# Opening of a two-layer diffusion-transformer kernel: key and value weights by feature quarter, modulation columns tile by tile, squares in two chains, decay table later

## The chip, the cores and the metric

The kernel runs on one core of a Trainium2 chip. A core has a matrix engine (TensorE, PE in the profile; PEld are its weight loads), three engines for elementwise work (VectorE is DVE, ScalarE is ACT, GpSimd is POOL), a queue engine that issues transfers (SyncE, SP) and 16 DMA engines. The metric is the device time of one launch in microseconds (us). Lower is better.

## The reference

Two layers over 512 latent tokens (x) with a prefix of 256 context tokens (ctx), model width 1024. Layer 0 mixes tokens with windowed grouped-query attention, layer 1 with a bidirectional retention; each is followed by a gated feed-forward stage. The part that this case is about is the head of layer 0: modulation from a condition vector, the modulated norm, and the projection to keys and values.

```python
def rms_norm(x, g):
    xf = x.astype(jnp.float32)
    y = xf * lax.rsqrt(jnp.mean(xf * xf, axis=-1, keepdims=True) + EPS)
    return (y * g.astype(jnp.float32)).astype(x.dtype)

def modulate(h, shift, scale):
    return h * (1 + scale) + shift

# windowed_gqa_sink
    q_x, k_x, v_x = jnp.split(h_x @ w_qkv, [qd, qd + kvd], axis=-1)
...
    k_c, v_c = jnp.split(h_c @ w_qkv[:, qd:], 2, axis=-1)
...
# bidir_retention
    log_g = jax.nn.log_sigmoid(decay_logit.astype(f32))
...
# reference
    c_act = jax.nn.silu(c)[:, None, :]
    cc_act = jax.nn.silu(c_ctx)[None, None, :]
    y_ctx = ctx
    for i in range(DEPTH):
        mx = jnp.split(c_act @ ada_w[i] + ada_b[i], 6, axis=-1)
        mc = jnp.split(cc_act @ ada_w[i] + ada_b[i], 6, axis=-1)
        h_x = modulate(rms_norm(x, norm1_g[i]), mx[0], mx[1])
        h_c = modulate(rms_norm(y_ctx, norm1_g[i]), mc[0], mc[1])
...
```

## The kernel before

Features lie on the 128 partitions, tokens on the free axis; the model width is eight feature tiles k = 0..7, and a *feature quarter* q is the pair 2q, 2q+1. Stream s = 0 is latent (512 columns), s = 1 context (256). Every float32 product is made of three matmuls, from a high part (a cast, on ScalarE) and a low part (the difference, on VectorE) of both operands: high by high, low weight by high, high weight by low.

The opening computes keys and values of all tokens, one feature quarter after the other, as their modulation comes. Its loads stand in SP's program order from line 334 on: four tiles of modulation weights for a quarter (`ada_quarter_load`), weight chunks for keys and values (`load_w`), the context stream, rope table, masks, the first query chunk, and the tiles of four later modulation units (`unit_load`, `UNITS` = 4, 5, 8, 6 at line 28; the first of them has buffers of its own). All modulation tiles and two of the weight chunks share eight buffers ("adan"), so a load waits until an earlier tile has been read. SP issues in program order; a load that waits holds what is behind it. Of the four chunks of 512 KB, chunk 0 and 1 hold the key weights of head pair 0 and 1 for all features, chunk 2 and 3 the value weights of the first and the last two feature quarters.

For TensorE, VectorE and ScalarE the order is written out by hand between line 469 and 517: within this block each of them runs its instructions in program order. Outside it a planner orders them, by priority.

- `stats0` (line 423, with `add_square` and `rms`): squares of the eight latent tiles on ScalarE, summed by seven additions on VectorE into one tile, then a matmul with ones, and from it the factor (`neg_half_rstd`, line 194: three ScalarE steps, two on VectorE at lines 199 and 200). Filler matmuls (`busy`, line 415) run meanwhile.
- `ada_quarter` (line 337): 64 matmul passes (line 345) give the modulation rows of a quarter in one PSUM bank; ScalarE copies them (348), `fill` runs, TensorE transposes twice (352), VectorE adds the bias and folds the gain (`columns`, 358, 359 and 114) for stream 0; the function it returns does stream 1.
- `hidden0` (line 429): scales two tiles (VectorE, 438), adds the shift into the high part (ScalarE, 439), then the low part (VectorE, 443). `between` runs ahead of the low parts.
- `split_w` (line 380) and `split_low` (384): high and low parts of a whole weight chunk.
- `keys` (line 445) and `values` (line 455): the matmuls of one quarter. For a quarter and a head pair, the latent keys are six passes of 512 columns, and there are two head pairs. A value tile is 128 tokens.
- `ada_unit` (line 311): as a quarter, for one later unit; passes at line 315.

The decay table of layer 1 (lines 787 to 809) is 21 small VectorE operations on 8 columns. It stands outside the hand-written block, behind two ScalarE steps. Layer 1 reads it. The first feed-forward stage (22 tiles f, in groups; `seven` computes one tile f from the third on) comes after layer 0's attention.

Of the kernel before, what the change touches and what calls it, by code (L numbers as in the profile page):

```python
# [9 lines left out]
F32R = mybir.dt.float32r  # L10
BF16 = mybir.dt.bfloat16
AF = mybir.ActivationFunctionType
ALU = mybir.AluOpType
# [36 lines left out]
def dit_kernel(ctx, tc, xT, cT, crow, small, consts, masks, tabs0, tabs1, jtab, adaQ, adaN, adaT, wst, out):  # L50
# [165 lines left out]
    def rms(s, c=slice(None), bank=pj, behind=()):  # L216
        y = ssq[s][:, c]
        n = y.shape[1]
        tot = bank()[:, :n]
        after(nc.tensor.matmul(tot, ones, y, start=True, stop=True), behind)  # L220
        return neg_half_rstd(y, t_sq(n), tot, D)
# [142 lines left out]


# [14 lines left out]
    def split_w(pool):  # L380
        wkv.append((T(pool, 1024, "whi", 2, F32R), T(pool, 1024, "wlo", 2, F32R)))
        nc.scalar.copy(wkv[-1][0], raw[len(wkv) - 1])

    def split_low():
        i = lows.pop(0)
        nc.vector.tensor_tensor(wkv[i][1], raw[i], wkv[i][0], op=sub)

    lows = [0, 1, 2, 3]
# [3 lines left out]
    load_w(rp, "wraw", 2)  # L392
    load_w(rp, "wraw", 2)
    load_w(st_p, "adan", 8)
    wq.append(ada_quarter_load(1))
    res0[1] = load_stream(1)
    load_w(st_p, "adan", 8)
    wq += [ada_quarter_load(2), ada_quarter_load(3)]
# [20 lines left out]
    def squares0(s):  # L419
        for k in range(KT):  # L420
            add_square(s, k, res0[s][k], tmp=(lambda n: T(st_p, 512, "hs", 3)[:, :n], lambda n: T(st_p, SC, "sc", 2)[:, :n])[s])

    def stats0(s):
        squares0(s)
        cond_silu(ccol)
        ln_exp_turn()
        rms(s, bank=pT)

    def hidden0(s, *ks, between=()):
        y, ts = ssq[s], []  # L430
        for k in ks:
# [13 lines left out]
    def keys(s, q):  # L445
        for j in range(2):
            o = kvx[j] if s == 0 else kvc[:, j * SC:(j + 1) * SC]
            for i, (a, b) in enumerate(((0, 0), (1, 0), (0, 1))):
                for k in (2 * q, 2 * q + 1):
                    last = nc.tensor.matmul(o, wkv[j][a][:, k * P:(k + 1) * P], h[s][k][b],  # L450
                                            start=k + i == 0 and (s == 0 or j == 0),
                                            stop=k == KT - 1 and i == 2, skip_group_check=s == 1)
        return last

    def values(s, q, tiles=None):
        first = None
        for t in tiles or ((0, 1, 2, 3), (4, 5))[s]:
            tok = slice((t - 4 * s) * P, (t - 4 * s) * P + P)
            o = kvv[t // 2][:, t % 2 * 256:t % 2 * 256 + 256]
            for k in (2 * q, 2 * q + 1):  # L460
                cs = slice((k % 4) * 256, (k % 4) * 256 + 256)
                (whi, wlo), (hi, lo) = wkv[2 + q // 2], h[s][k]
# [6 lines left out]
    with tc.manual_schedule(engines={mybir.EngineType.PE, mybir.EngineType.DVE, mybir.EngineType.Activation}):  # L469
        for n in (SX, SX, SX, SX, 256):  # L470
            busy(n)
        stats0(0)
        c1 = ada_quarter(0, wq[0], lambda: busy(256))
        split_w(st_p)
        busy(SX)
        hidden0(0, 0, 1, between=(split_low,))
        c1()
        split_w(st_p)
        split_low()
        keys(0, 0)  # L480
# [24 lines left out]
        c1()  # L505
# [288 lines left out]
    nc.vector.tensor_scalar(t2, t1, 2.0, None, op0=add)  # L794
    nc.vector.reciprocal(t2, t2)
    nc.vector.tensor_tensor(t1, t1, t2, op=mult)
    nc.vector.tensor_tensor(t2, t1, t1, op=mult)
    NTERM = 10
    nc.vector.tensor_scalar(t3, t2, 1.0 / (2 * NTERM + 1), None, op0=mult)
    for k in range(NTERM - 1, 0, -1):  # L800
# [1118 lines left out]
```

## Time and profile before

| | us |
|---|---|
| median of 3 runs | 1747.07 |
| lowest, highest run | 1746.09, 1747.19 |
| the profiled execution | 1746.2 |
| its span in the trace | 1744.4 |
| TensorE busy in it | 1712.7 (98%) |
| VectorE busy | 1350.5 (77%) |
| ScalarE busy | 846.3 (49%) |
| transfers | 203.54 MB, mean 117 GB/s |

A row of a timeline gives the start in us from the span's start, the length, the engine, the line of the kernel, the operation, the tile written and those read, the shape, a count where several instructions of a kind stand in a row, and in brackets the idle time before it with what ended it. A row of a table by stretches gives the stretch, then for each engine its busy time and number of instructions, then the TensorE clock that was granted (1.00 is full), the share of the DMA engines and GB/s. A row on waits gives engine and line, what it waited for, the total, the count and the longest. The chain of waits follows the work that ended last back through what released it. Matmuls overlap, so rows of TensorE are compared by their starts.

### The profile page before, as it was taken

How to read it: one execution, taken by the hardware profiler on the slowest of the kernel's cores; microseconds unless marked ns; L12 is line 12 of the kernel's file. 1: busy time of each engine (PE TensorE's matmuls, PEld its weight loads, DVE VectorE, ACT ScalarE, POOL GpSimd, SP SyncE). 2: the span in 40 equal slices, each digit the busy share in tenths (PEclk: the TensorE clock that was granted, in tenths of full speed). 3: DMA queues.
4: the chain of work that ended last, by engine and by line, in shares of the span. 5: the costliest groups of instructions: out<-in, count | busy, mean ns of one | idle time of the engine just before them, and what ended most of it. 6: DMA issues, size and time to landing. Idle time of an engine off the chain costs nothing.

```text
span 1744.4 us, 27605 instructions
## 1 busy us (share of the span) xinstructions
PE 1712.7 (98%) x10876; PEld 1527.8 (88%) x10876; DVE 1350.5 (77%) x2368; ACT 846.3 (49%) x1492; POOL 131.0 (8%) x270
## 2 busy tenths in 40 slices
PE   7999999999999999999999999999999999999999
PEld 5777777899999999999988888898898899999997
DVE  6697778788778788787889858758768798777774
ACT  5576667465433334342456534525525565445442
POOL 0035435000000000000000000000000000000000
PEclk9999999999999999999999999999999999999999
DMA  9501012533243534343423524423423224233322
GB/s 353 230 13 38 13 43 68 204 122 135 71 147 121 158 109 145 123 153 101 156 99 86 182 84 130 162 86 121 157 85 118 76 84 132 77 117 101 104 79 85
DMA packets 59602, 203.54 MB, mean 117 GB/s; under 512 B 6608, under 2 KB 6992, under 8 KB 59216
## 3 DMA queue, kind: packets, MB, share of 16 engines
q1 hardware_dynamic: 51984, 175.03, 30.9%
q0 software_dynamic: 7200, 26.22, 5.2%
q8 instruction: 85, 1.39, 0.3%
q10 hardware_dynamic: 288, 0.52, 0.1%
q14 instruction: 45, 0.37, 0.1%
HBM read 199.65 MB, written 2.10 MB: 116 GB/s over the span
## 4 chain that ended last, share of the span: by engine, by line
PE 80%; DVE 8%; DMA 5%; ACT 3%; issue 2%; POOL 1%; SPq 0%; ACTq 0%; POOLq 0%; DVEq 0%
PE Y L886 15%; PE Z L886 7%; PE pj L147 6%; PE pj L148 6%; PE pj L149 6%; PE Z L1268 6%; PE X L886 4%; PE Y L1257 3%; PE pj L1268 2%; PE pT L726 2%; PE X L1257 2%; DMA wraw<-in_wst_dram 2%; PE pO L740 2%; PE S L703 2%; DMA adan<-in_adaQ_dram 1%
## 5 line engine op out<-in xcount | busy, mean ns | idle before, releaser
L164 ACT CAST whi<-wraw 128x1024 fp32r<-128x1024 f32 x258 | 270.2, 1051 | 370.7 <-PE Z L149 88.5
L165 DVE TENSOR_TENSOR wlo<-wraw,whi 128x1024 fp32r<-128x1024 f32 x258 | 315.0, 1223 | 60.9 <-ACT whi L164 59.7
L886 PE MATMUL Y<-aq,whi 128*128 128x384 f32 x640 | 173.7, 335 | 0.5 <-ACT sq L1044 0.5
L256 DVE SCALAR_TENSOR_TENSOR res<-pj,mod,res 128x512 f32<-128x512 f32 (+1 forms) x112 | 81.5, 729 | 65.6 <-PE pj L149 65.0
L886 PEld LDWEIGHTS Y<-aq,whi 128*128 128x128 f32 x640 | 116.6, 188 | 1.7 <-ACT sq L1044 0.9
L273 DVE CUSTOM_DVE_ANT_0 y<-adaw,crow,small_sb 128x1024 bf16<-128x1024 f32 x64 | 81.9, 1280 | 36.0 <-DMA adaw<-in_adaT_dram 35.7
L886 PE MATMUL Y<-aq,wlo 128*128 128x384 f32 x320 | 107.0, 334 | 0.0
L101 ACT ACTIVATE pr<-pr,stat,qs 128x513 f32<-128x513 f32 (+2 forms) x96 | 74.4, 777 | 23.5 <-DVE stat L710 22.9
L1268 PE MATMUL Z<-whi,sA 128*128 128x512 f32 x256 | 81.0, 391 | 1.2 <-ACT gate L1454 1.2
L717 POOL TENSOR_SCALAR pr<-pr,stat 128x512 f32<-128x512 f32 (+2 forms) x96 | 70.2, 744 | 79.5 <-DVE stat L714 54.8
L147 PE MATMUL pj<-ax,whi 128*128 128x512 f32 x176 | 68.8, 391 | 0.1
L149 PE MATMUL pj<-ax,whi 128*128 128x512 f32 x176 | 68.7, 390 | 0.0
L148 PE MATMUL pj<-ax,wlo 128*128 128x512 f32 x176 | 68.5, 389 | 0.0
L147 PE MATMUL pj<-act,whi 128*128 128x512 f32 x168 | 66.0, 393 | 0.0
L148 PE MATMUL pj<-act,wlo 128*128 128x512 f32 x168 | 65.9, 392 | 0.0
L149 PE MATMUL pj<-act,whi 128*128 128x512 f32 x168 | 65.5, 390 | 0.0
L270 POOL DMA_DIRECT2D adaw<-in_adaT_dram x48 | 25.6, 533 | 514.9 <-DVE mod L273 413.6
L726 PE MATMUL pT<-const_sb,pr 128*128 128x128 f32 x352 | 57.4, 285 | 6.1 <-POOL pr L717 3.6
L886 PE MATMUL Y<-sA,whi 128*128 128x256 f32 x304 | 60.6, 282 | 0.2 <-ACT res L1721 0.2
L886 PEld LDWEIGHTS Y<-aq,wlo 128*128 128x128 f32 x320 | 60.1, 188 | 0.0
L726 PEld LDWEIGHTS pT<-const_sb,pr 128*128 128x128 f32 x352 | 39.1, 142 | 23.0 <-POOL pr L717 12.4
L1268 PEld LDWEIGHTS Z<-whi,sA 128*128 128x128 f32 x256 | 48.0, 188 | 11.7 <-ACT gate L1454 1.9
(576 smaller groups left out, 5150.3 us busy)
## 6 DMA issues: line engine op xcount, KB each, us to landing
wraw<-in_wst_dram SPq DMA_DIRECT2D x224, 512.0 KB, 3.7
adaw<-in_adaT_dram POOLq DMA_DIRECT2D x48, 512.0 KB, 3.9
wx<-in_wst_dram SPq DMA_DIRECT2D x30, 512.0 KB, 4.3
adan<-in_adaQ_dram SPq DMA_DIRECT2D x16, 512.0 KB, 8.5
adan<-in_adaN_dram SPq DMA_DIRECT2D x12, 512.0 KB, 7.8
adaw<-in_adaT_dram SPq DMA_DIRECT2D x8, 512.0 KB, 3.9
res<-in_xT_dram SPq DMA_DIRECT2D x14, 256.0 KB, 3.8
aq<-in_adaN_dram SPq DMA_DIRECT2D x12, 256.0 KB, 5.8
```

The source lines that it names most:

```text
L101: ins = nc.scalar.activation(*args, **kw)
L147: nc.tensor.matmul(o, whi, xhi, start=first, stop=False)
L148: nc.tensor.matmul(o, wlo, xhi, start=False, stop=False)
L149: return nc.tensor.matmul(o, whi, xlo, start=False, stop=last)
L164: after(nc.scalar.copy(hi, t), behind)
L165: return nc.vector.tensor_tensor(lo, t, hi, op=sub)
L256: return nc.vector.scalar_tensor_tensor(res[d], o, mods[l, s][:, part, d:d + 1], res[d], mult, add)
L273: res.append(nc.vector.tensor_tensor_reduce(junk, w, cr[:, s * 1024:(s + 1) * 1024], 1.0, sm_t[:, C_ADAB + l * 48 + j:C_ADAB + l * 48 + j ...
L726: nc.tensor.transpose(tp[:, a * P:(a + 1) * P], self.pr[(0, 2, 1, 3)[a]][:, ki * P:(ki + 1) * P], ident)
L886: nc.tensor.matmul(o, p, r, start=first and k + i == 0, stop=k == 3 and i == 2, skip_group_check=not first)
L1257: ins = nc.tensor.matmul(o[:, e * SC:(e + 1) * SC], p[:, ws], r, start=first and k + e + i == 0, stop=k == 3 and i == 2, skip_group_check= ...
L1268: ins = nc.tensor.matmul(os[t], p, r, start=first and k + i == 0, stop=k == 3 and i == 2, skip_group_check=by_k or not first)
```

## The change

1. `rms` can sum several tiles by ones (`rest`). `stats0` keeps two running sums, for even and odd tiles: six additions in place of seven, and two matmuls with ones. One short filler matmul is left out.
2. The key and value weights are stored by feature quarter: chunk q holds, for tiles 2q and 2q+1, the key weights of both head pairs (columns 0 to 511) and the value weights (512 to 1023). `split_high` and `split_low` take a column range; quarters 0 and 1 are split in halves (keys, values), quarters 2 and 3 whole.
3. The order of loads: quarter 0's modulation tiles, chunk 0, quarter 1's tiles, chunk 1, the context stream, quarter 2's tiles, chunk 2, quarter 3's tiles, chunk 3. Chunks 0 and 1 have buffers of their own, as the first two had; chunks 2 and 3 take one of the eight.
4. `ada_tiles` takes the place of `ada_quarter` for quarters 0 and 1: the quarter's two tiles one after the other, each with its 32 passes, its copy, a `fill` and its transpose, both transposes into one bank. The weights of these two quarters are stored to suit. Columns are added tile by tile, each ahead of its tile's scaling (`ahead` of `hidden0`).
5. `keys` can run part by part (`by_part`): all high passes, then all low-weight passes, then all low-hidden passes.
6. The hand-written order follows: the context squares stand behind the second quarter's low parts, the context factor in the fill of the third modulation quarter, two value tiles of quarter 1 ahead of it. `split_low(2)` stands where the last `split_low()` stood; `split_high(3)` behind the last latent `hidden0`, `split_low(3)` behind the last context one.
7. The VectorE part of the decay table becomes `decay`, called in the first feed-forward stage behind tile f = 12.

```diff
-    def rms(s, c=slice(None), bank=pj, behind=()):
+    def rms(s, c=slice(None), bank=pj, behind=(), rest=()):
...
-        after(nc.tensor.matmul(tot, ones, y, start=True, stop=True), behind)
+        for i, t in enumerate((y, *rest)):
+            after(nc.tensor.matmul(tot, ones, t, start=i == 0, stop=i == len(rest)), behind)
...
+    def ada_tiles(q, w, fill):
+        t = None
+        for d in range(2):
+            o = pT()[:, 0:P]
+            for k2 in range(4):
+                for j in range(4):
+                    k = 2 * k2 + j % 2
+                    nc.tensor.matmul(o[32 * j:32 * j + 32, :], ccol[:, k, :], w[2 * d + j // 2][:, k * P:(k + 1) * P],
+                                     start=k2 == 0, stop=k2 == 3)
+            rows = t_sq(P)
+            nc.scalar.copy(rows, o)
+            fill[d]()
+            if t is None:
+                t = pT()[:, 0:256]
+            nc.tensor.transpose(t[:, d * P:(d + 1) * P], rows, ident)
...
+        def columns(s, d0, d1):
+            col = mods[0, s][:, 0:2, 2 * q + d0:2 * q + d1]
+            nc.vector.tensor_tensor(col, tv[:, s, 0, :, d0:d1], bias[:, :, d0:d1], op=add)
+            nc.vector.tensor_tensor(col, tv[:, s, 1, :, d0:d1], col, op=add)
+            fold_gain(0, s, 0, 2 * q + d0, 2 * q + d1)
+
+        return columns
...
+    def split_high(q, c=slice(0, 1024)):
+        if q == len(wkv):
+            pool = (st_p, rp)[q // 2]
+            wkv.append((T(pool, 1024, "whi", 2, F32R), T(pool, 1024, "wlo", 2, F32R)))
+        nc.scalar.copy(wkv[q][0][:, c], raw[q][:, c])
+
+    def split_low(q, c=slice(0, 1024)):
+        nc.vector.tensor_tensor(wkv[q][1][:, c], raw[q][:, c], wkv[q][0][:, c], op=sub)
...
     load_w(rp, "wraw", 2)
+    wq.append(ada_quarter_load(1))
     load_w(rp, "wraw", 2)
-    load_w(st_p, "adan", 8)
-    wq.append(ada_quarter_load(1))
     res0[1] = load_stream(1)
-    load_w(st_p, "adan", 8)
-    wq += [ada_quarter_load(2), ada_quarter_load(3)]
+    for q in (2, 3):
+        wq.append(ada_quarter_load(q))
+        load_w(st_p, "adan", 8)
...
+    def stats0():
+        ssq[0] = t_y(0)
+        sums = ssq[0], t_sq(SX)
+        for k in range(KT):
+            sq = sums[k] if k < 2 else T(st_p, 512, "hs", 3)
+            nc.scalar.activation(sq, res0[0][k], AF.Square)
+            if k > 1:
+                nc.vector.tensor_tensor(sums[k % 2], sums[k % 2], sq, op=add)
         cond_silu(ccol)
         ln_exp_turn()
-        rms(s, bank=pT)
+        rms(0, bank=pT, rest=sums[1:])
...
-        for n in (SX, SX, SX, SX, 256):
+        for n in (SX, SX, SX, SX):
             busy(n)
-        stats0(0)
-        c1 = ada_quarter(0, wq[0], lambda: busy(256))
-        split_w(st_p)
+        stats0()
+        columns = ada_tiles(0, wq[0], [lambda: busy(256), lambda: (split_high(0, KEYS), busy(256))])
         busy(SX)
-        hidden0(0, 0, 1, between=(split_low,))
-        c1()
-        split_w(st_p)
-        split_low()
-        keys(0, 0)
-        split_w(rp)
-        split_low()
-        squares0(1)
-        c1 = ada_quarter(1, wq[1], lambda: values(0, 0, (0, 1)))
-        hidden0(0, 2, 3)
-        c1()
+        hidden0(0, 0, 1, between=[lambda: split_high(0, VALUES), lambda: split_low(0, KEYS)],
+                ahead=[lambda d=d: columns(0, d, d + 1) for d in range(2)])
+        keys(0, 0, by_part=True)
+        columns(1, 0, 2)
+        split_low(0, VALUES)
+        columns = ada_tiles(1, wq[1], [lambda: values(0, 0, (0,)), lambda: (split_high(1, KEYS), values(0, 0, (1,)))])
+        hidden0(0, 2, 3, between=[lambda: split_high(1, VALUES), lambda: split_low(1, KEYS)],
+                ahead=[lambda d=d: columns(0, d, d + 1) for d in range(2)])
         values(0, 0, (2, 3))
-        rms(1, bank=pT)
-        keys(0, 1)
-        c1 = ada_quarter(2, wq[2], lambda: values(0, 1, (0, 1)))
+        split_low(1, VALUES)
+        columns(1, 0, 2)
+        squares1()
+        keys(0, 1, by_part=True)
+        values(0, 1, (0, 1))
+        c1 = ada_quarter(2, wq[2], lambda: (rms(1, bank=pT), values(0, 1, (2,))))
         c1()
         hidden0(1, 0, 1)
-        split_w(rp)
+        split_high(2)
         hidden0(1, 2, 3)
-        values(0, 1, (2, 3))
+        values(0, 1, (3,))
         c1 = ada_quarter(3, wq[3], lambda: (keys(1, 0), hidden0(0, 4, 5)))
         c1()
-        split_low()
+        split_low(2)
         keys(1, 1)
         hidden0(0, 6, 7)
+        split_high(3)
         keys(0, 2)
         c1 = ada_unit(UNITS[0], wu[0])
         hidden0(1, 4, 5)
         hidden0(1, 6, 7)
+        split_low(3)
         c1()
...
+                if f == 12:
+                    decay([end])
...
-    for j in range(2):
-        ch.append(_cols(qkv, 1024 + 128 * j, 128))
-    wv = qkv[:, 1280:1536].reshape(KT, P, 256).transpose(1, 0, 2)
-    ch += [wv[:, 0:4].reshape(P, 1024), wv[:, 4:8].reshape(P, 1024)]
+    wk = qkv[:, 1024:1280].reshape(4, 2, P, 256).transpose(0, 2, 1, 3).reshape(4, P, 512)
+    wv = qkv[:, 1280:1536].reshape(4, 2, P, 256).transpose(0, 2, 1, 3).reshape(4, P, 512)
+    ch += [np.concatenate([wk[i], wv[i]], axis=1) for i in range(4)]
...
+    adaQ[0:2] = (ada_w[0, :, :2048].reshape(KT, P, 2, 4, 2, P)[:, :, :, 0:2].transpose(3, 4, 2, 1, 0, 5)
+                 .reshape(2, 2, 2, P, D))
```

More of the change, by code (lines that the diff above doesn't have):

```diff
@@ L378, in load_w @@
         wpos[0] += 1
[L380 to L388, printed above, removed]
+    KEYS, VALUES = slice(0, 512), slice(512, 1024)
+    def split_high(q, c=slice(0, 1024)):
[5 more added lines that the diff above has]
+        nc.vector.tensor_tensor(wkv[q][1][:, c], raw[q][:, c], wkv[q][0][:, c], op=sub)
     wkv = []
@@ L460, in values @@
             for k in (2 * q, 2 * q + 1):
-                cs = slice((k % 4) * 256, (k % 4) * 256 + 256)
-                (whi, wlo), (hi, lo) = wkv[2 + q // 2], h[s][k]
+                cs = slice(512 + k % 2 * 256, 768 + k % 2 * 256)
+                (whi, wlo), (hi, lo) = wkv[q], h[s][k]
                 for i, (a, b) in enumerate(((hi, whi), (hi, wlo), (lo, whi))):
```

62 lines of the change are left out of this document (34 added, 28 removed).

## Prediction, made before the change was run

> **What bounds the kernel now.** First the page: its span, and TensorE's share slice by slice.
>
> ```profile
> span 1744.4 us, 27605 instructions
> PE   7999999999999999999999999999999999999999
> ```
>
> TensorE is full in every slice but the first (43.6 us), so what the opening can give back is what TensorE idles there. The chain of waits over the first 110 us says for what it idles (start, length, what):
>
> ```profile
> 6.62 5.62 DMA adan<-in_adaQ_dram
> ...
> 34.75 0.62 PE pT L345 x16
> 35.77 1.64 SPq L400
> ...
> 50.52 10.19 DMA adan<-in_adaN_dram
> 60.75 0.64 PE pT L315 x16
> ```
>
> Modulation tiles rotate through eight buffers. The last feature-quarter tile needs one that TensorE frees at 34.75 + 0.62; SP stands at it, the rope table goes out only at 35.77, and at 50.52 + 10.19 = 60.71 the transfer lands that lets TensorE finish the third late modulation unit. Stretch by stretch (DMA share and GB/s are the last columns):
>
> ```profile
> 32.00:34.00 2.00, 2.00 (x9) 1.63 (x10) 1.85 (x6) 1.06 (x3) 0.00 (x0) 1.00 1.04 424
> 34.00:36.00 2.00, 2.00 (x52) 1.59 (x54) 0.04 (x1) 0.00 (x0) 0.00 (x0) 1.00 0.69 277
> 36.00:38.00 2.00, 2.00 (x36) 1.80 (x28) 0.00 (x0) 0.37 (x1) 0.00 (x0) 1.00 0.77 213
> 38.00:40.00 2.00, 2.00 (x24) 1.87 (x26) 1.34 (x8) 0.03 (x1) 0.00 (x0) 1.00 0.74 188
> 40.00:42.00 2.00, 2.00 (x66) 1.80 (x60) 1.82 (x5) 1.99 (x4) 0.00 (x0) 1.00 0.96 332
> ```
>
> Against 424 GB/s the stretches from 34 to 42 miss 147 + 211 + 236 + 92 = 686 GB/s for 2 us, or 3.2 us of transfer time. That hole is the most that better traffic alone can give.
>
> TensorE's timeline, for prices and marks:
>
> ```profile
> 12.50 1.12 PE L220 MATMUL pT<-y,ones_sb 128*128 128x512 f32 x2 [1.02 <-DVE y L213]
> 24.61 1.96 PE L345 MATMUL pT<-adan,ccol 128*32 128x128 f32 x64
> 34.68 1.96 PE L345 MATMUL pT<-adan,ccol 128*32 128x128 f32 x64
> 39.85 1.96 PE L345 MATMUL pT<-adan,ccol 128*32 128x128 f32 x64
> 48.11 1.56 PE L315 MATMUL pT<-k,ccol 128*32 128x128 f32 x48
> 60.75 0.64 PE L315 MATMUL pT<-adan,ccol 128*32 128x128 f32 x16 [0.59 <-DMA adan<-in_adaN_dram]
> 61.32 0.73 PE L450 MATMUL pj<-h,whi 128*128 128x512 f32 x2
> 64.18 0.40 PE L450 MATMUL pO<-hc,whi 128*128 128x256 f32 x2
> ```
>
> Marks: first latent key quarter done 24.6, second 34.7, third 48.1, third late unit 61.3. From 61.32 on TensorE is dense, so its shift there is the kernel's. Prices: twelve 512-wide key passes 64.18 - 61.32 = 2.86, 0.24 each; a modulation quarter or unit 1.9, half of it 0.95; four value tiles with two transposes 39.85 - 36.6 = 3.25, some 0.75 a tile.
>
> The other rows that the sum uses, the last one from the page's DMA issues (512 KB land 3.7 us after their issue when nothing is ahead):
>
> ```profile
> 5.89 5.59 PE L417 MATMUL kvv<-res,ones_sb 128*128 128x512 f32 x10 [5.89 <-DMA res<-in_xT_dram]
> 6.96 5.48 DVE L213 TENSOR_TENSOR y<-y,hs 128x512 f32<-128x512 f32 x7 [2.11 <-ACT hs L212]
> 13.66 0.69 ACT L101 ACTIVATE y<-pT,small_sb 128x512 f32<-128x512 f32 x1 [1.08 <-PE pT L220]
> 13.67 1.77 DVE L801 SCALAR_TENSOR_TENSOR lg_t<-lg_t,lg_t 128x8 f32<-128x8 f32 x9
> 16.47 0.69 DVE L200 SCALAR_TENSOR_TENSOR y<-sq,y 128x512 f32<-128x512 f32 x1
> 17.37 0.15 DVE L358 TENSOR_TENSOR mod<-pT,small_sb 128x4 f32<-128x4 f32 x1
> 17.95 1.41 DVE L438 SCALAR_TENSOR_TENSOR hs<-res,acol,y 128x512 f32<-128x512 f32 x2
> 25.85 3.07 DVE L213 TENSOR_TENSOR y<-y,sc 128x256 f32<-128x256 f32 x6 [0.53 <-ACT sc L212]
> 39.46 0.87 DVE L438 SCALAR_TENSOR_TENSOR hs<-res,acol,y 128x256 f32<-128x256 f32 x2
> 46.98 1.22 DVE L386 TENSOR_TENSOR wlo<-adan,whi 128x1024 fp32r<-128x1024 f32 x1
> 71.18 0.66 ACT L164 CAST pr<-wraw 128x512 fp32r<-128x512 f32 x1
> 74.23 0.68 DVE L165 TENSOR_TENSOR pr<-wraw,pr 128x512 fp32r<-128x512 f32 x1
> ...
> wraw<-in_wst_dram SPq DMA_DIRECT2D x224, 512.0 KB, 3.7
> ```
>
> **The change part by part.** I lay each engine's instructions behind one another in the new order, with these durations, and note when each mark comes.
>
> *Loads.* SP issues the same bytes in another order: one chunk of four serves the first keys, where two did, and the last two go behind the third and fourth modulation quarters. No load is needed sooner than it came: nothing won or lost but the place of the hole.
>
> *Squares in two chains.* Seven dependent additions take 5.48, 0.78 each, and end at 12.44. Six remain, whose neighbours belong to different sums; independent operations of this size run at about 0.65 (L438, two in 1.41, with latency). From the third square, near 7.5, they end near 11.2. TensorE multiplies two sums by ones (0.85 each plus latency) behind fillers that, without the short fifth, end at 10.9: the total stands at 12.75, and it was 13.6. The factor (L200's end, 17.16) comes at 16.3.
>
> *Decay table later.* Four of its operations stand in VectorE's list just ahead of the columns at 17.37; at the pace of the L801 row they took at most 0.8 us, and that much is freed.
>
> *Columns tile by tile.* Does the first tile's column wait for the second tile's transpose? Both land in one PSUM bank, and no row shows this case. The nearest is an eviction of two halves of one bank:
>
> ```profile
> 278.69 0.29 DVE L165 TENSOR_TENSOR hc<-pO,hc 128x128 fp32r<-128x128 f32 x1
> 279.01 0.27 ACT L164 CAST hc<-pO 128x128 fp32r<-128x128 f32 x1 [0.18 <-DVE hc L165]
> ```
>
> ScalarE, at the second half, waits for VectorE's read of the first: a bank is handed over whole. I take it that the columns wait for both transposes; were it otherwise, 0.6 us are won here and as much in the second quarter (bound below). The first transpose needs the copy of its rows behind ScalarE's three factor steps (15.0) and a bank, the second tile's 0.95 us of matmuls follow on TensorE, then copy and transpose: 17.35, no sooner than before. Columns and scaling, now twice one after the other, take 0.55 + 0.7 + 0.5 + 0.7: 19.8, and ScalarE's high part ends at 20.5. What is won lies in the halves: 0.66 and 0.68 split the keys' weights in the gaps. With low parts last, the first keys run three high passes, four, four: 23.2, and it was 24.6.
>
> *Second quarter.* TensorE does half a quarter, value tile, transpose, twice (0.95 + 0.75 + 0.2): 27.0. The same 2.5 us on VectorE, high part 0.7: 30.2, eleven passes: 32.9, and it was 34.7. Two value tiles that stand ahead of the third modulation quarter now take 1.5; the quarter runs 34.4 to 36.3, where it ran 34.68 to 36.6. So SP gets its buffer 0.3 us sooner, two tiles wait for buffers where one did, and the hole stays.
>
> *Context statistics.* Their additions sat in the old second quarter's gaps; now VectorE has them behind the low parts (31.4), half a weight low (0.65) and the context columns (0.55): seven at 0.51 (the row at 25.85) end at 36.1. Then ones matmul 0.6 behind the quarter's (36.9), three ScalarE steps 1.4, two VectorE operations 0.9, both column sets 0.95. The first context scaling starts at 40.2; it was 39.46. **All that was won is spent, and 0.75 more.**
>
> *Third key quarter.* From that scaling to the end of the low part at 46.98, VectorE runs a sequence of 48.20 - 39.46 = 8.74 us in the same order as before: it ends at 48.95. Before, this low part was for later values; now it holds the third quarter's key weights. TensorE does two high passes and stands from 46.2 to 48.95. Behind its waiting pass are the first late unit, the context values and the second unit, and behind that unit's buffers the last four loads. Ten passes later it is 51.4, where it was 48.1.
>
> From there TensorE has no more reason to wait for transfers: unit and copy 2.45 (it took 3.3 with waits for data), values 3.0, unit 1.9, context keys 1.5, transpose 0.2, unit 1.9, together 10.95: 62.35 against 61.32. One more wait: the fourth chunk's raw tile holds one of the eight buffers until its low part, last in VectorE's list at about 58.2 (four steps of 0.85 behind the copy at 53.65, then 1.2). If the eighth late tile gets that buffer it lands at 61.9, just when TensorE wants it. Loss 1.1.
>
> *The decay table's new place.* 21 operations, 3.8 us at the 0.2 of the L801 row, enter VectorE's list in the first feed-forward stage:
>
> ```profile
> 658.00:665.50 7.50, 7.50 (x45) 7.50 (x44) 6.71 (x11) 4.21 (x7) 0.53 (x1) 1.00 0.66 185
> 665.50:673.00 7.50, 7.50 (x45) 7.50 (x45) 6.54 (x12) 2.53 (x4) 0.53 (x1) 1.00 0.32 94
> DVE y L273 <- DMA adaw<-in_adaT_dram: 4.8, 3, 3.7
> ```
>
> VectorE is 13.25 of 15 us busy there and TensorE never waits; between 650 and 690 VectorE idles 4.8 us for modulation weights (last row), which hides the table. Cost 0 if it does, 3.8 if not; I take 0.1.
>
> **Sum.** +1.1 + 0.1 = +1.2. The profiled execution took 1746.2 (span 1744.4 and 1.8 around it), 0.9 under the median of the runs: 1747.4 in its own time, 1748.3 as a median.
>
> **Rivals.**
>
> *The bank is not handed over whole* (faster). 0.6 and 0.7 sooner in the two quarters move the context scaling to 38.5 and everything behind it: the unit is done near 60.65, a gain of 0.6: 1746.5. For it: the change is laid out for it. Against: the wait at 279.01.
>
> *Transfers stay the bound and go better* (faster). If the statistics end 3 us sooner, the third unit comes with its data and the hole shrinks: a gain of 2.6 to the full 3.2, 1744.5 to 1743.9. For it: the chain is made of transfers. Against: the 8.74 us on VectorE.
>
> *The decay table costs.* VectorE has 1.75 us of room in those 15. What goes over stalls TensorE; half hidden, 1.9: 1750.1; nothing hidden: 1752.0.
>
> *TensorE gets cold.* Its first passes were slow:
>
> ```profile
> 5.80:8.60 2.80, 2.71 (x4) 1.19 (x5) 1.42 (x3) 2.80 (x6) 0.00 (x0) 1.00 1.02 386
> 8.60:11.40 2.80, 2.80 (x8) 1.28 (x6) 2.49 (x4) 2.45 (x5) 0.00 (x0) 1.00 1.05 410
> ```
>
> Four passes in the first stretch, eight in the next, at the same granted 1.00. The stand of 2.75 us could bring that state back: a loss of 1.4 more, as in that stretch, 1749.7. The Trainium skill (TensorE: Matmul & The Clock Gate, "What's actually happening") says that an idle window of about 3.4 us halves the rate; by that rule this stand stays short of it, and no pause of this opening after the first work, 1.0 us at 12.50 among them, can test it.
>
> **How the numbers follow.** The forecast has 0.50, the bank 0.20, transfers 0.08, decay 0.12, cold 0.10. The range 1744.7 to 1750.4 leaves out the transfers and the far half of the decay case. About 0.2% (3.5 us) is what a measurement tells from no change. Under 1743.6: only past the transfers' hole, 0.05. Over 1750.6: most of the decay case and a little of the cold one, 0.11. Within: 0.84. The likeliest case alone spans 1747.3 to 1749.2, 1 us either way for the start of the context scaling.
>
> **What would show it.** Right: no decay operations before 17 us; columns behind both transposes; second key quarter done near 33; a TensorE wait of 2 to 3 us for a low weight part ahead of the third quarter's keys, near 46 to 49; no wait for data over 0.5 us in the third late unit, done near 62.4. Wrong: context scaling before 39, no wait for the low part, the unit done by 60; or TensorE waiting between 658 and 690.

## The result, and the profile after

The changed kernel takes 1755.50 us (median of 6 runs, 1755.18 to 1757.71) where the kernel before, beside it on the same chip, takes 1746.98: a ratio of 1.0049, with a 95% interval of 1.0039 to 1.0059. It is 8.5 us slower. The forecast was 1748.3 in a range up to 1750.4: the time lies outside. The profiled execution is the longest of the six, 1757.71 with a span of 1755.9, which is 11.5 us over the span before. Of these 11.5, 3.0 belong to the two profiled executions and not to the kernels: this one is 2.2 us over its median, and that of the kernel before was 0.8 us under.

The page of the changed kernel: span, TensorE's share and the granted clock, slice by slice.

```profile
span 1755.9 us, 27628 instructions
...
PE   7999999999999999999999999999999999999999
...
PEclk9989999999999999999999999999999999999999
```

TensorE looks as full as before, but the third slice (88 to 132 us) has a clock of 8. Nothing on the page's other lines shows 11 us; the time is found by laying marks side by side. TensorE's timeline of the changed kernel:

```profile
12.47 1.02 PE L221 MATMUL pT<-y,ones_sb 128*128 128x512 f32 x2
...
17.17 1.08 PE L374 MATMUL pT<-adan,ccol 128*32 128x128 f32 x32 [0.24 <-DVE sq L199]
...
18.72 0.33 PE L381 MATMUL pT<-const_sb,sq 128*128 128x128 f32 x1
...
36.92 1.96 PE L346 MATMUL pT<-adan,ccol 128*32 128x128 f32 x64
...
51.47 0.73 PE L491 MATMUL pj<-h,wlo 128*128 128x512 f32 x2 [2.35 <-DVE wlo L417]
...
53.18 1.05 PE L491 MATMUL pj<-h,wlo 128*128 128x512 f32 x2
...
55.02 2.46 PE L316 MATMUL pT<-k,ccol 128*32 128x128 f32 x64
...
66.31 0.74 PE L491 MATMUL pj<-h,whi 128*128 128x512 f32 x2
```

The third modulation quarter starts at 36.92 (34.68 before). The third quarter's keys wait 2.35 us for a low part, and the passes behind that wait are slow: the last four before the unit at 55.02 take 1.84 us from 53.18 on, where four took 0.95, and that unit of 64 passes takes 2.46, where 64 took 1.96. The third late unit is done at 66.31, where it was done at 61.32. So the opening lost 5.0 us. VectorE's timeline at the same places:

```profile
10.82 0.69 DVE L460 TENSOR_TENSOR sq<-sq,hs 128x512 f32<-128x512 f32 x1
...
17.15 0.69 DVE L200 SCALAR_TENSOR_TENSOR y<-sq,y 128x512 f32<-128x512 f32 x1
19.09 0.16 DVE L387 TENSOR_TENSOR mod<-pT,small_sb 128x2 f32<-128x2 f32 x1 [1.24 <-PE pT L381]
...
42.69 0.87 DVE L476 SCALAR_TENSOR_TENSOR hs<-res,acol,y 128x256 f32<-128x256 f32 x2
...
50.20 1.22 DVE L417 TENSOR_TENSOR wlo<-adan,whi 128x1024 fp32r<-128x1024 f32 x1
```

But 5.0 is not 11.5. Counting TensorE's instructions from the end of both traces tells how late the changed kernel is at a given amount of work left: 5.1 us where the kernel before stands at 85 us, 10.1 at its 440 and 650, 10.4 at its 690, 11.5 at the end. A second loss of 5 us lies between 85 and 130 us, in the first attention stages, where the diff touches nothing. TensorE's waits there (engine and line, what it waited for, total, count, longest), in the stretch from 44 to 125 us of the changed kernel:

```profile
PE pj L491 <- DVE wlo L417: 2.3, 1, 2.3
PE pj L652 <- ACT sq L627: 1.9, 1, 1.9
PE pj L147 <- ACT whi L164: 1.8, 1, 1.8
```

Before, the longest wait in that stretch was one of 0.7. The third row is TensorE waiting for a high part of weights of the second query stage. ScalarE's timeline has that cast; the first fence is the kernel before, the second the changed one:

```profile
71.69 1.10 ACT L164 CAST whi<-wraw 128x1024 fp32r<-128x1024 f32 x1
```

```profile
95.56 1.03 ACT L164 CAST whi<-wraw 128x1024 fp32r<-128x1024 f32 x1
```

It comes 24 us later. Its weights use the buffers in which `split_high(2)` and `split_high(3)`, with their low parts, put chunks 2 and 3, and this first cast takes those of chunk 2. Before, chunk 2 held the value weights of the first two quarters and its last reader was the context values of the second quarter, near 54 us; now chunks 2 and 3 are the third and fourth quarter, and their last readers are the context values that stand behind the whole first query stage. The hold is not the whole of the wait: by the order of the passes chunk 2 is read for the last time near 93.4 us, and ScalarE then makes four casts of query parts, from 93.30 to 95.42, ahead of this one.

### The profile page after: what moved, and what is told of

Same layout as the page of the kernel before. It is cut to its first block, busy times and chain, and to the rows that moved or that the text cites. A ratio compares the mean times of both kernels' runs of the same rounds, so it can differ in the third digit from the quotient of the medians.

```text
span 1755.9 us, 27628 instructions
## 1 busy us (share of the span) xinstructions
PE 1722.2 (98%) x10878; PEld 1535.5 (87%) x10878; DVE 1349.4 (77%) x2375; ACT 846.8 (48%) x1496; POOL 129.6 (7%) x270
## 4 chain that ended last, share of the span: by engine, by line
PE 78%; DVE 11%; DMA 4%; ACT 4%; issue 2%; POOL 1%; SPq 0%; ACTq 0%; DVEq 0%; POOLq 0%
PE Y L930 14%; PE Z L930 7%; PE pj L147 7%; PE pj L148 6%; PE pj L149 6%; PE Z L1314 4%; PE X L930 3%; DVE wlo L165 2%; DMA wraw<-in_wst_dram 2%; PE pT L768 2%; PE X L1303 2%; PE Y L1303 2%; PE S L745 2%; PE pO L782 2%; PE pj L1314 2%
## 5 line engine op out<-in xcount | busy, mean ns | idle before, releaser
L759 POOL TENSOR_SCALAR pr<-pr,stat 128x512 f32<-128x512 f32 (+2 forms) x96 | 66.3, 704 | 84.4 <-DVE stat L756 74.2
L746 DVE CUSTOM_DVE_ANT_0 pr<-S,mask,qs 128x256 f32<-128x256 f32 (+1 forms) x96 | 52.9, 567 | 9.7 <-PE S L745 8.3
```

## Experiments

Theory A: the opening loses by a low part of chunk 2 that comes late, with a low clock behind it, and the first attention stages lose by buffers that are held too long. Rivals: B, the decay table and the order that the planner makes with it; C, transfers of the late units take the place of whatever wait is removed; others are named with their runs. All ratios are to the kernel before, run beside each; a difference between two runs of the table carries the width of both intervals.

| run | edit | ratio (95% interval) |
|---|---|---|
| | changed kernel | 1.0049 (1.0039 to 1.0059) |
| e1_release | context values earlier | 1.0020 (1.0011 to 1.0029) |
| e2_vfirst | context values of quarter 0 in the gap | 1.0038 (1.0026 to 1.0051) |
| e3_decay_early | decay table back | 1.0048 (1.0035 to 1.0060) |
| e4_before_hold | kernel before, buffers held | 1.0000 (0.9991 to 1.0008) |
| e5_rel_c2 | e1, chunk 2 split early | 1.0002 (0.9993 to 1.0011) |
| e6_rel_stats | e1, context statistics early | 1.0021 (1.0012 to 1.0030) |
| e7_rel_both | e1, both | 1.0007 (0.9998 to 1.0016) |
| e8_rel_quarter | e1, modulation by whole quarters | 1.0006 (0.9997 to 1.0015) |
| e9_rel_c2_quarter | e5, modulation by whole quarters | 0.9992 (0.9983 to 1.0001) |
| e10_c2_alone | changed, chunk 2 split early | 1.0033 (1.0020 to 1.0046) |
| e11_before_chains | kernel before, squares in two chains | 0.9999 (0.9990 to 1.0008) |

**e1_release.** The context values move ahead of the last query tile.

```diff
         after(values(0, 2), [last_key])
+        values(1, 2)
...
         values(0, 3)
-        q0[3]()
-        values(1, 2)
         values(1, 3)
+        q0[3]()
```

> The changed kernel with one move: the context values of the third quarter stand right behind its latent values, those of the fourth right behind its latent values, both ahead of the last query tile of that stage (the same matmuls). So the high and low parts of chunks 2 and 3 have their last reader earlier and their buffers come free earlier. Theory A (part of the loss is a buffer that is held: the query tiles of the second stage wait for high parts that cannot be written, 1.78 us at 96.64 in the changed kernel, and TensorE's clock falls behind it): the high part for that stage is cast 2 to 5 us sooner, the waits at 96.64 and 110.80 shrink, and the kernel comes 3 to 4 us under the changed one, 1751.5 to 1752.5. Rival B (the loss behind 70 us comes from the planner's other order with the decay table moved): within 1 us of the changed kernel, 1755.5.

Measured: 1.0020 for 1.0049, 5.1 us less. ScalarE's timeline of this run has the cast 18.5 us sooner:

```profile
77.01 1.10 ACT L164 CAST whi<-wraw 128x1024 fp32r<-128x1024 f32 x1
```

TensorE's waits of this run from 44 to 125 us:

```profile
PE pj L147 <- DVE qs L655: 1.2, 1, 1.2
PE pj L652 <- ACT sq L627: 0.7, 1, 0.7
```

The wait for the cast is gone, that at L652 is 0.7 instead of 1.9, and one of 1.2 for VectorE's part of the query factors has come in. Counted from the end the run is 4.0 us late at the 85 us of the kernel before and 4.1 at its 440: the second loss has vanished. The gain is more than the 1.8 us by which these waits shrank and more than the 3 to 4 us expected, since the low clock behind the waits went as well (last section). Theory A holds for this half; B, which expected no effect, falls. The move does two things at once, though: it frees the buffers sooner, and it changes the order of TensorE's own work in this stage.

**e3_decay_early.** The decay table is made at its old place.

```diff
         nc.vector.tensor_scalar(dcol[:, 3, :], lg[:, 4:8], -1.0, None, op0=mult)
+    decay([])
...
-                if f == 12:
-                    decay([end])
```

> The changed kernel with the decay table back at its early place, as in the kernel before; all else as changed. Theory A (the loss is the opening's order and the held buffers): 1755 to 1756, the same as the changed kernel within 1 us. Rival B (the decay table in the first feed-forward stage, or the planner's other order that comes with it, costs the 4 to 6 us that appear behind 67 us): 1750 to 1752.

Measured 1.0048: nothing. Theory A's figure, and B is out. The traces agree: in the stretch of the first feed-forward stage TensorE is busy throughout. First the kernel before, then the changed one:

```profile
650.00:690.00 40.00, 40.00 (x229) 39.27 (x228) 33.26 (x51) 18.91 (x31) 2.64 (x5) 1.00 0.52 154
```

```profile
650.00:690.00 40.00, 39.95 (x230) 39.50 (x230) 36.87 (x76) 19.98 (x32) 2.64 (x5) 1.00 0.43 132
```

VectorE does 3.6 us more there, and TensorE is still busy 39.95 of 40.

**e4_before_hold.** The buffers held in the order of before.

```diff
         values(1, 3)
+        held = pT()[:, :256]
+        for i in range(2):
+            nc.tensor.matmul(held, wkv[2][i][:, 0:P], h[0][0][0][:, 0:256], start=i == 0, stop=i == 1)
```

> The kernel before with two more short matmuls behind the last context values, which read the high and the low part of chunk 2 and whose sum nobody uses: they hold that chunk's buffers as long as the changed kernel does, and are themselves 0.25 us of work. Theory A (held buffers delay the next stage's high parts): the cast of the second stage's high part falls from 71.69 to past 80, TensorE waits for it, and the kernel is 2 to 4 us slower than before, 1749 to 1751. Rival B, and rival D (the buffers are held but other work covers it): 0.3 us slower, 1747.3.

Measured 1.0000: theory A missed here, rival D was right. The cast did fall late, as expected, but TensorE hardly waited. ScalarE's and TensorE's timelines of this run:

```profile
91.06 1.05 ACT L164 CAST whi<-wraw 128x1024 fp32r<-128x1024 f32 x1
```

```profile
91.08 0.51 PE L706 MATMUL S<-k,q 128*128 128x256 f32 x2 [0.52 <-DVE q L601]
...
92.15 0.50 PE L147 MATMUL pj<-h,whi 128*128 128x512 f32 x1 [0.21 <-ACT whi L164]
...
93.59 0.50 PE L148 MATMUL pj<-h,wlo 128*128 128x512 f32 x1 [0.59 <-DVE wlo L165]
```

Between the last reader and the first use TensorE has rope and score matmuls to do, and none of these waits is longer than 0.6. So a held buffer alone costs nothing: it costs where the order leaves TensorE nothing to do in the 2 us between the last read of the old weights and the high part of the new. In the changed kernel it stands there for 1.78. ScalarE's four query casts stand ahead of the high part in both (88.25 to 90.36 here), so they are not what differs; TensorE's filling work is. Why the planner found it in one order and not in the other was not tried.

**e2_vfirst.** On the changed kernel, work for the gap.

```diff
         split_high(3)
+        values(1, 0)
         keys(0, 2)
...
         c1()
-        values(1, 0)
         values(1, 1)
```

> The changed kernel with one move on TensorE: the context values of the first quarter (two tiles, twelve short passes, 1.5 us as their rows show) stand ahead of the latent keys of the third quarter, where TensorE waits 2.35 us for the low part of chunk 2 at 51.47. Theory A (this wait and the half clock from 52.7 to 56.1 behind it are 3 to 4 us of the opening's loss of 5.0): the wait shrinks to under 1 us, the clock stays at 1.00 there, and the kernel comes 2 to 3.5 us under the changed one, 1752 to 1753.5. Rival C (the low part is no bound: what TensorE reads next is late too, so that a wait of the same length appears at the next unit): within 1 us of the changed kernel. Rival B (planner's order with the decay table) expects 1755.5 as well.

Measured 1.0038, 1.9 us less than the changed kernel with intervals that overlap: just short of the 2 to 3.5 that theory A expected, and not clear of noise. The wait fell to 1.5 and the clock stayed at 1.00, but the late units then waited for data. TensorE's waits of this run from 44 to 125 us:

```profile
PE pT L316 <- DMA adan<-in_adaN_dram: 2.4, 3, 1.4
...
PE pj L491 <- DVE wlo L417: 1.5, 1, 1.5
```

Rival C has a part in it: what was won by filling the gap was partly spent waiting for data further on.

**e5_rel_c2.** On e1, the two parts of chunk 2 go where VectorE stands idle.

```diff
         squares1()
+        split_high(2)
+        split_low(2)
         keys(0, 1, by_part=True)
...
         hidden0(1, 0, 1)
-        split_high(2)
...
         c1()
-        split_low(2)
         keys(1, 1)
```

> The kernel of e1_release (context values earlier) with the high and low part of chunk 2 moved forward in the order, right behind the context squares, where VectorE stands idle 2.48 us until 39.66 in that run; before, the low part ended at 50.1 behind the context tiles and TensorE waited 2.34 us for it at 50.17. Same operations. Theory A (what the opening still loses, some 4 us, is this late low part and the half clock that follows the wait): the wait goes, the clock stays at 1.00 from 48 to 56, the third late unit is done 3 to 4 us sooner as far as its data allow (they land at 61.01), and the kernel is 3 us under e1_release, ratio to before 0.9995 to 1.001. Rival C (the transfers of the late units hold TensorE in place of it): under 1.5 us, ratio 1.001 to 1.002.

Measured 1.0002, 3.1 us under e1: the whole loss is back. VectorE's and TensorE's timelines of this run:

```profile
37.39 1.23 DVE L417 TENSOR_TENSOR wlo<-adan,whi 128x1024 fp32r<-128x1024 f32 x1 [0.36 <-ACT whi L414]
```

```profile
47.55 0.62 PE L491 MATMUL pj<-h,wlo 128*128 128x512 f32 x2
...
61.88 0.64 PE L316 MATMUL pT<-adan,ccol 128*32 128x128 f32 x16 [0.59 <-DMA adan<-in_adaN_dram]
62.46 0.73 PE L491 MATMUL pj<-h,whi 128*128 128x512 f32 x2
```

The low part is ready 9 us ahead of its use, the wait of 2.34 is gone, and now the third late unit waits for its last tile and is done at 62.46 (65.02 in e1). Theory A, with rival C as the next bound.

**e10_c2_alone.** The same edit on the changed kernel, without e1's.

> The changed kernel with chunk 2's two parts early alone; the context values stay at the end of the first query stage. Theory A (two causes that are nearly independent: the late low part, some 3 us, and the held buffers, some 3.5 us): 3 to 4 us under the changed kernel's ratio of 1.0049, so 1.0025 to 1.0032, with TensorE still waiting 1.8 us for the high part near 92. Rival F (the two causes are one: without the first delay the second stage's weights come in time): 1.0002 to 1.001, as e5_rel_c2.

Measured 1.0033: 2.8 us under the changed kernel, just short of the 3 to 4 that theory A expected and with intervals that overlap, and TensorE's wait for the high part is still there. Rival F is out. TensorE's waits of this run from 12 to 125 us:

```profile
PE pj L652 <- ACT sq L627: 1.9, 1, 1.9
PE pj L147 <- ACT whi L164: 1.8, 1, 1.8
```

The two causes add up: the place of the context values is worth 5.1 us with the late low part and 5.4 without it (1.0033 to 1.0002), the late low part 2.8 and 3.1. Together some 8.2 of the 8.5.

**e6_rel_stats and e7_rel_both.** On e1, the context statistics early; e7 has e5's edit too, with the two parts behind the columns.

```diff
         split_low(0, VALUES)
+        squares1()
...
         split_low(1, VALUES)
+        rms(1, bank=pT)
         columns(1, 0, 2)
-        squares1()
...
-        c1 = ada_quarter(2, wq[2], lambda: (rms(1, bank=pT), values(0, 1, (2,))))
+        c1 = ada_quarter(2, wq[2], lambda: values(0, 1, (2,)))
```

> The kernel of e1_release with the context squares back behind the first value weights' low part (VectorE idles 4.68 us there until 28.09) and the context factor behind the second quarter's low parts, as in the kernel before. Same operations. Theory A (the prediction's step that the context statistics, put behind, delay the context scaling): the first context scaling starts 1.5 to 2.5 us sooner than 41.39, the low part of chunk 2 as much sooner than 50.1, TensorE's wait for it falls below 1 us, and the kernel is 2 to 3 us under e1_release, ratio 1.0003 to 1.001. Rival C (transfers): under 1 us.

> The kernel of e1_release with both moves: context squares and factor early, and chunk 2's two parts right behind them. Theory A: the wait for the low part is gone and the context scaling sooner as well; TensorE reaches the third late unit when its data do, so the two moves do not add up: 3 to 4.5 us under e1_release, ratio 0.999 to 1.0005, at best a shade faster than the kernel before. Rival C: no better than e5_rel_c2 and e6_rel_stats, ratio 1.001.

Measured 1.0021 and 1.0007: no gain over e1 and over e5. Theory A's step on the context statistics falls in the main. VectorE's and TensorE's timelines of e6:

```profile
40.67 0.16 DVE L359 TENSOR_TENSOR mod<-pT,small_sb 128x4 f32<-128x4 f32 x1 [4.20 <-PE pT L353]
...
41.60 0.87 DVE L476 SCALAR_TENSOR_TENSOR hs<-res,acol,y 128x256 f32<-128x256 f32 x2
```

```profile
50.38 0.73 PE L491 MATMUL pj<-h,wlo 128*128 128x512 f32 x2 [2.35 <-DVE wlo L417]
```

With the statistics done early, VectorE idles 4.20 us and then waits for the third quarter's own modulation: the scaling starts at 41.60 (41.39 in e1, whose factor came 1.03 sooner). Counted from the end of the latent factor that is 0.8 us sooner than in e1, not the 1.5 to 2.5 expected; TensorE's keys come sooner too, and wait 2.35 us for the low part as before. The statistics were not the only thing that held the scaling.

**e8_rel_quarter.** On e1, whole quarters again, with the split halves in the same places; the second quarter likewise, and the weights stored as before.

```diff
-        columns = ada_tiles(0, wq[0], [lambda: busy(256), lambda: (split_high(0, KEYS), busy(256))])
+        c1 = ada_quarter(0, wq[0], lambda: (split_high(0, KEYS), busy(256)))
         busy(SX)
-        hidden0(0, 0, 1, between=[lambda: split_high(0, VALUES), lambda: split_low(0, KEYS)],
-                ahead=[lambda d=d: columns(0, d, d + 1) for d in range(2)])
+        hidden0(0, 0, 1, between=[lambda: split_high(0, VALUES), lambda: split_low(0, KEYS)])
         keys(0, 0, by_part=True)
-        columns(1, 0, 2)
+        c1()
```

> The kernel of e1_release with the modulation of the first two quarters made as in the kernel before: the whole quarter in one run of 64 passes, columns of both tiles together; all else as there. Theory A (the bank is handed over whole, so that tile by tile wins nothing): the factor of the first tile's columns comes no later, VectorE has three small operations less in each quarter (0.5 us), and the kernel is within 1 us of e1_release, ratio 1.0015 to 1.0025. Rival E (tile by tile does win, because the first tile's scaling starts while the second's columns wait): 1 to 2 us slower, ratio 1.0027 to 1.003.

Measured 1.0006, 2.4 us under e1, with intervals that just overlap. Theory A said within 1 us, so it missed, and rival E is wrong in sign: tile by tile costs. VectorE's timelines, first e1, then e8:

```profile
15.90 0.69 DVE L200 SCALAR_TENSOR_TENSOR y<-sq,y 128x512 f32<-128x512 f32 x1
17.83 0.16 DVE L387 TENSOR_TENSOR mod<-pT,small_sb 128x2 f32<-128x2 f32 x1 [1.24 <-PE pT L381]
...
19.66 0.75 DVE L476 SCALAR_TENSOR_TENSOR hs<-res,acol,y 128x512 f32<-128x512 f32 x1
```

```profile
17.31 0.69 DVE L200 SCALAR_TENSOR_TENSOR y<-sq,y 128x512 f32<-128x512 f32 x1
17.92 0.15 DVE L359 TENSOR_TENSOR mod<-pT,small_sb 128x4 f32<-128x4 f32 x1
...
18.50 1.42 DVE L476 SCALAR_TENSOR_TENSOR hs<-res,acol,y 128x512 f32<-128x512 f32 x2
```

From the end of the factor to the end of the second scaling it takes 20.41 - 16.59 = 3.8 us tile by tile and 19.92 - 18.00 = 1.9 by quarters. Made whole, the quarter's modulation is finished while ScalarE works on the factor. Tile by tile, the second tile's passes wait until VectorE has read the sum of squares (L374 at 17.17 in the changed kernel, 0.24 us behind "DVE sq L199"), so half the modulation, its copy and its transpose come behind the factor's first VectorE step. The traces confirm the sign: from the factor's end to the third modulation quarter it takes 19.0 us in e1 (16.59 to 35.63) and 16.2 in e8 (18.00 to 34.24).

**e9_rel_c2_quarter.** e5 with e8's edit, both as shown above.

> The kernel of e5_rel_c2 (context values earlier, chunk 2 split early) with the first two quarters' modulation made whole, as in e8_rel_quarter. Theory A (tile by tile costs the opening 2.8 us between the factor and the third modulation quarter, because the second tile's passes wait for a PSUM bank that VectorE reads at the end of the factor; and the loads behind the hole at 28 to 36 us come as much sooner when that quarter runs sooner): the third modulation quarter starts 1.4 us sooner than in e5_rel_c2, its buffer comes free and the late units' tiles land about 1.4 us sooner, and the kernel is 1 to 2 us under e5_rel_c2, ratio 0.9988 to 0.9997: a shade faster than the kernel before. Rival C (the late units' transfers are full already, so that nothing behind them moves): ratio 0.9998 to 1.0006, as e5_rel_c2.

Measured 0.9992 (0.9983 to 1.0001), median 1745.67 beside 1747.39: the quickest of all, though its interval just reaches 1 and overlaps that of e5. TensorE's timeline of this run:

```profile
33.59 1.96 PE L346 MATMUL pT<-adan,ccol 128*32 128x128 f32 x64
...
59.59 0.64 PE L316 MATMUL pT<-adan,ccol 128*32 128x128 f32 x16 [0.59 <-DMA adan<-in_adaN_dram]
60.16 0.73 PE L491 MATMUL pj<-h,whi 128*128 128x512 f32 x2
```

The third modulation quarter starts 1.9 us sooner than in e5 (35.52 there), its buffer comes free as much sooner, and the late unit, still waiting for its last tile, is done at 60.16, 1.2 us ahead of the kernel before. This is the path that the change was near: earlier buffers, hence earlier transfers.

**e11_before_chains.** The kernel before with `stats0` and `rms` as in the change.

```diff
-        for n in (SX, SX, SX, SX, 256):
+        for n in (SX, SX, SX, SX):
...
-        squares0(s)
+        ssq[0] = t_y(0)
+        sums = ssq[0], t_sq(SX)
+        for k in range(KT):
+            sq = sums[k] if k < 2 else T(st_p, 512, "hs", 3)
+            nc.scalar.activation(sq, res0[0][k], AF.Square)
+            if k > 1:
+                nc.vector.tensor_tensor(sums[k % 2], sums[k % 2], sq, op=add)
...
-        rms(s, bank=pT)
+        rms(s, bank=pT, rest=sums[1:])
```

> The kernel before with one part of the change alone: squares in two chains, six additions for seven, two matmuls with ones, one short filler less. Theory A (the opening of the kernel before is bound by transfers behind the hole, so a factor that comes 1 us sooner wins nothing at the third late unit): ratio 0.9995 to 1.0004. Rival G (the factor is on the path): 0.5 to 1 us faster, 0.9994 to 0.9997; a filler less costs clock: 0.5 to 1 us slower, 1.0003 to 1.0006.

Measured 0.9999: nothing, as theory A said. TensorE's timeline of this run ends the third late unit where the kernel before did:

```profile
61.31 0.73 PE L457 MATMUL pj<-h,whi 128*128 128x512 f32 x2
```

## Why the prediction was wrong

**Squares in two chains**: right. The additions end at 11.51 (forecast 11.2). The factor's end was forecast at 16.3 and is 17.84 in the profiled execution, but 16.59 in e1, which has the same opening. TensorE's first passes got fast later in the one than in the other: between 8.6 and 11.4 us it has four passes in the changed kernel and seven in e1, and the trace's record of the granted clock begins at 11.74 and at 9.43. (In the kernel before it begins at 8.89. A stretch without a record counts as full, so the 1.00 that the prediction read beside its slow first passes is not a measurement.) e11 shows that none of it reaches the end.

**Decay table**: right. Forecast 0.1; e3 and the stretch from 650 to 690 show no more.

**Columns tile by tile**: the mechanism was right, the weighing wrong. The columns did wait for both transposes (19.09, right behind the second at 18.72), and they came no sooner than before. But the working compared this with the kernel before, and so hid a price: it had 3.5 us from the factor to the second scaling and never asked what whole quarters would need with the same earlier factor (1.9). e8 puts the part at 2.4 us, with the noise said above. The rival of a bank that is not handed over whole did not come.

**Context statistics**: "All that was won is spent, and 0.75 more" gave 40.2 for the first context scaling; it was 42.69, and 41.39 in e1. The profiled execution is 2.5 us behind the forecast here, and it was so already at the end of the second key quarter (35.4 for 32.9); 1.5 of it are the late factor. That the statistics were the main cause is not borne out: e6 moves them away, and behind the factor the scaling comes only 0.8 us sooner.

**Third key quarter**: right in kind and size, a wait of 2.35 for the low part where 2.75 was forecast, and no wait for data behind it, as forecast. The third late unit was put at 62.35 and is done at 66.31. About 1.3 us of these 4.0 are the late start of this execution (17.84 less 16.59), 1.2 the steps up to the scaling that were sized too short (41.39 less 40.2), and the rest, about 1.5, the low clock: the rival *TensorE gets cold*, held at 0.10 and priced at 1.4, came true along with the forecast, since the same wait brings both. They should not have been given separate chances.

**The step that failed** is the sentence "From 61.32 on TensorE is dense, so its shift there is the kernel's." At the third late unit the shift is 5.0; at the 440 us of the kernel before it is 10.1. The working followed the buffers of the opening's loads, but not those in which chunks 2 and 3 lie when they have been split. With the new meaning of the chunks their last reader moved from the opening to the end of the first query stage, and the next stage's weights use the same buffers. e1 takes 5.1 us back by moving that reader forward in the stage. e4 shows that the hold by itself, in the order of before, costs nothing: the loss is a hold together with an order that leaves TensorE idle behind it, and why the order does so stays open. A step for this stood in neither the sum nor the rivals.

Without this loss the changed kernel is at 1.0020, near 1750.5, a shade over the upper end of the range. So a term of the sum was too small as well: the opening's loss, put at 1.1, is some 3.5 us there. What it left out is above: the price of tile by tile beside whole quarters, and the low clock behind the wait for the low part.

## What to carry to other kernels

When a change regroups data in a buffer, list the last reader of every buffer in the pool before and after, also those whose next user lies in a later stage: a buffer that is held longer can show up as a wait far from the edit, where the order leaves an engine nothing else to do. A mark behind which TensorE is dense carries a shift to the end only if the work that comes in behind it finds its buffers as free as before. And a part that is "no sooner than before" can still be a loss, where another part of the same change would have brought it sooner: price each part against the kernel with all the others.

## What was not expected of the hardware

One wait does not always cost the same, because of the granted clock. The wait for chunk 2's low part is 2.35 us in the changed kernel, 2.34 in e1 and 2.35 in e6; behind it the clock falls to a half in the first two and stays full in e6. Stretches of 3.41 us, laid so that their edges fall on the clock's changes, show a difference. Columns: stretch, then for TensorE, its weight loads, VectorE, ScalarE and GpSimd the busy time and count, then granted clock, transfers' share and GB/s. The changed kernel, with the waits of the attention stage too:

```profile
49.29:52.70 3.41, 1.23 (x5) 1.05 (x6) 3.27 (x10) 0.59 (x1) 0.00 (x0) 1.00 1.06 408
52.70:56.12 3.42, 3.42 (x30) 2.35 (x32) 2.25 (x5) 1.73 (x3) 0.00 (x0) 0.50 1.02 417
93.66:97.08 3.42, 1.64 (x12) 1.18 (x10) 3.25 (x7) 3.33 (x9) 0.00 (x0) 1.00 0.00 0
97.08:100.49 3.41, 3.26 (x12) 2.82 (x12) 3.29 (x10) 2.15 (x4) 0.37 (x2) 0.50 0.36 91
107.32:110.73 3.41, 1.58 (x14) 1.37 (x13) 2.30 (x4) 2.18 (x5) 1.00 (x1) 1.00 0.01 2
110.73:114.15 3.42, 3.35 (x13) 3.16 (x14) 3.29 (x9) 2.61 (x8) 0.00 (x0) 0.50 0.00 0
```

Then e6, whose wait from 48.03 to 50.38 lies across such an edge:

```profile
45.50:48.91 3.41, 2.38 (x16) 1.68 (x14) 3.17 (x9) 1.39 (x2) 0.00 (x0) 1.00 1.05 395
48.91:52.32 3.41, 1.94 (x8) 1.61 (x9) 3.24 (x6) 1.29 (x3) 0.00 (x0) 1.00 1.05 411
52.32:55.74 3.42, 2.67 (x69) 2.04 (x67) 1.67 (x4) 1.51 (x4) 0.00 (x0) 1.00 1.03 420
```

A stretch in which TensorE is busy 1.23, 1.58 or 1.64 us is followed by one at half clock; one with 1.94 is not. So the wait of 2.35 us was followed by 3.4 us at half clock where it fell inside one stretch, or nearly (the changed kernel, e1), and by none where an edge cut it (e6). Busy time alone does not decide it: in the kernel before, the stretch from 15.71 to 19.13 us has 1.70 busy and the next one keeps the full clock, and in e11 the one from 121.86 to 125.27 has 2.24 and the next one is at half. What else counts these runs do not show. The Trainium skill (TensorE: Matmul & The Clock Gate, "What's actually happening") describes a free-running window of 3413 ns, and the stretches agree with that (the half clock of the changed kernel sets in at 52.70, 97.08 and 110.73, 13 and 4 such windows apart), with the run-to-run chance that it implies. It asks for an idle window of about that length; here a window that was idle for a little over half was enough, and the prediction's sentence that this wait "stays short of it" took the rule too literally. The same chance is in the start: the factor of one and the same opening ended at 16.59 in e1 and at 17.84 in the changed kernel's profile.
